# A transformer layer with 32 experts on one core: the skipped general pass and the norm's spread at other experts, chunks taken by pairs of pages

## The chip, the cores and the metric

The kernel runs on one core of a Trainium2 chip. The metric is the device time of one execution in microseconds (us). It has five engines that matter here: TensorE (PE, with its weight loads as PEld), VectorE (DVE), ScalarE (ACT), GpSimd (POOL) and SyncE (SP). In this kernel SP issues every transfer between the outer memory and the core's own memory.

## The reference, cut to what matters

One decoder layer for 256 tokens of width 1024: attention and a gated recurrence, an output projection, a layer norm, then a mixture of 32 experts of which each token takes 4, then a second layer norm. All weights are float32. What bears on the change:

```python
h = layer_norm(DN_ALPHA * h + mix, ln1_g[l], ln1_b[l])
ffn = moe(h, w_router[l], b_router[l], w_gate_up[l], b_gate_up[l], w_down[l], b_down[l])
h = layer_norm(DN_ALPHA * h + ffn, ln2_g[l], ln2_b[l])
# in moe, for each expert e and the rows xb that chose it:
h = xb @ w_gu[e] + b_gu[e]                       # 1024 -> 2 x 1024
act = gate * jax.nn.sigmoid(SWIGLU_ALPHA * gate) * (up + 1.0)
y = act @ w_dn[e] + b_dn[e]                      # 1024 -> 1024, weighted and added per token
```

An expert has 8 MB of gate and up weights and 4 MB of down weights, so the 32 experts read about 403 million bytes, and each byte is used once.

## The kernel before, in words

The first part (projections, attention, recurrence, router) is put in order by a planner with costs and priorities; it ends at about 205 us of the profiled execution. The rest is a plain loop over the 32 experts, written in the order in which each engine runs it. This loop holds the change.

**Pages.** The core's memory for weights is a set of pages of 1 MB. Two neighbouring pages are one tile, called page0 to page12 in the rows; the profile leaves the number out. A queue of wanted loads is drained by `pump`, which is called whenever a buffer is freed while the program is being built. An expert's gate and up weights are eight chunks of 1 MB, g*e*_0 to g*e*_7, its down weights four, d*e*_0 to d*e*_3. In the loop `pump` prefers to load two chunks at once into two neighbouring pages (2 MB, line 436), which needs both pages of a tile to be free; otherwise a chunk goes alone (1 MB, line 451). After the first experts eleven tiles are in turn. SP waits for each load in the order of issue: for the last matmul that reads the old content of the tile, and for the landing of the load eight places earlier, since eight semaphores are shared in turn.

**One turn of the loop for expert e.** `gate_up` (line 1647): four small matmuls for the bias, then eight chunks of eight matmuls, then the gate on DVE and ACT. `down` of the expert before (line 1682): two for the bias, 32 matmuls. `turn` (line 1670) transposes the gated rows, `scatter_lhs` (line 1637) the weighted selection; on odd experts `gather` (line 1620) selects the tokens of the next two experts by matmuls with a 0/1 matrix; `combine` (line 1728) adds the outputs of the expert before into four accumulators. Every matmul goes through the helper at line 488, every transpose through line 495.

**What the change touches.** The first layer norm's gain and bias rows (`ln1`) are spread over the partitions by `spread` (two matmuls each) and applied to `h1` by `gain_bias` (line 1755, four DVE operations) at experts 0 and 1. The residual, `alid` times `h1`, is eight matmuls that start the four accumulators, at expert 1. `count` (line 1798) finds the largest number of tokens of any expert, at expert 0. `fallback` (line 1757) is a general pass for experts with more than 64 tokens, within a branch that all engines take or skip; with these inputs it is skipped. It stands at the last expert, 31, between `combine` of expert 29 and the first half of `gate_up` of 31. The last expert's loads come in pieces of 0.25 to 1 MB.

Of the kernel before, what the change touches and what calls it, by code (L numbers as in the profile page):

```python
# [34 lines left out]
SCRATCH = 1024  # L35
NR = 4
WARM = 30
GATE = {'wq0': 2.75, 'wq1': 5.75, 'wkg0': 8.75, 'wkg1': 11.5, 'wgh0': 14.5, 'wgh1': 17.5, 'wqa0': 20.25, 'wqa1': 23.25, 'wvs0': 26.25, 'wkv0': 29.0, 'wc00': 32.0, 'wc10': 35.0, 'wc01': 37.75, 'wc11': 40.75, 'wi0': 43.75, 'wi1': 46.5, 'wo2': 49.5, 'wo3': 61.75, 'wo0': 64.5, 'wo1': 69.75, 'bias': 86.0, 'xres': 87.5, 'ln1': 90.25, 'g0_0': 91.0, 'g0_1': 94.0, 'g0_2': 101.75, 'g0_3': 104.5, 'g0_4': 107.5, 'g0_5': 110.5, 'g0_6': 113.25, 'g0_7': 118.0, 'g1_0': 122.0, 'g1_1': 124.75, 'g1_2': 127.75, 'g1_3': 130.75, 'g1_4': 137.5, 'g1_5': 140.25, 'g1_6': 143.25, 'g1_7': 151.0, 'd0_0': 153.75, 'd0_1': 156.75, 'd0_2': 159.75, 'd0_3': 167.25}
# [284 lines left out]
def layer(ctx: ExitStack, tc: tile.TileContext, a: dict, out: bass.AP, dbg=None, n_exp=NEXP, cap_limit=CAP):  # L323
# [71 lines left out]
    def want(name, src, shape, kind="pre"):  # L395
        queue.append((name, src, shape, kind))

    def pump():
        while queue:
            name, src, shape, kind = queue[0]  # L400
# [969 lines left out]
    def router_sums():  # L1370

        yield ROUTER_AT
        scratch["late"][0] = Buf(0, key=(qf_late[0], 1024, 1024))
        rsum, gb1, wr1 = (brief(n_, [w], "late") for n_, w in (("rsum", 2 * NEXP), ("gb1", 2 * KD), ("wr1", (KD + 2) * NEXP)))
        wr1v, rsum = shaped(wr1, (KD, NEXP)), shaped(rsum, (2, NEXP))
        h1b.update(rsum=rsum, gb1=gb1, wr1=wr1)
        tmp, ones = brief("rtmp", [KD, NEXP]), brief("ones", [128], "late")
        sums = brief("sums", [2, NEXP], "late")
        pool.memset(ones, 1.0)
        fm = lambda c: col_of(c)[:, :, None].to_broadcast([P, KD, NEXP])  # L1380
        pool.tensor_tensor(tmp, wr, fm(B_B1), OP.mult)
        pool.tensor_tensor(wr1v, wr, fm(B_G1), OP.mult)
        pool.memset(wr1[:, KD * NEXP:], 0.0)
        pool.tensor_copy(gb1, pk[:, B_G1:B_G1 + 2 * KD])
        yield
        dve.tensor_reduce(sums[:, 0, :], tmp.rearrange("p k e -> p e k"), AX.X, OP.add)
# [50 lines left out]
    def norm_route(t):  # L1437
# [76 lines left out]
        h1b[f"tw{t}"] = (ts, tw)  # L1514

    def gather_first(t):

        yield f"rk{t}"
        yield "pm11" if t == 0 else "g0"
        if t == 0:  # L1520
            while (bk := grab(2)) is None:
                yield POLL
            h1b["pg"] = bk
        pg, gb1 = h1b["pg"], h1b["gb1"]
        for k in range(KD):
# [7 lines left out]
        for k in range(KD):  # L1533
            z, o = pg[k // 4][:, (k % 4) * 128:(k % 4 + 1) * 128], h1b["xg"].v(KD, 128)[:, k, :]
            if k % 2:
                act.activation(o, z, AF.Identity, bias=gb1[:, KD + k:KD + k + 1], scale=gb1[:, k:k + 1])
            else:
                dve.tensor_scalar(o, z, gb1[:, k:k + 1], gb1[:, KD + k:KD + k + 1], OP.mult, OP.add)
        drop(*pg)
# [79 lines left out]

    def gather(xg, G):  # L1620

        n = G.shape[2] * CAP
        for q in range(2):
            bk = take(1)
            for t in range(2):
                for k in range(4):
                    mm(bk[0][:, k * 128:k * 128 + n], h1[:, t, (4 * q + k) * 128:(4 * q + k + 1) * 128],
                       G[:, t].rearrange("p e s -> p (e s)"), k == 0 and t == 0, t == 1)
            act.copy(xg[:, 4 * q:4 * q + 4, :n], bk[0].rearrange("p (a b) -> p a b", a=4)[:, :, :n])  # L1629
            drop(*bk)  # L1630
# [15 lines left out]

    def gate_up(xg, wg, i3e, ga, sg_, fs=slice(0, FF)):

        hb = take(2)
        n = (fs.stop - fs.start) // 2  # L1650
        ones_ = i3e.to_broadcast([96, CAP])
        for k in range(-1, KD):
            w_ = wg(k) if k >= 0 else None
            for j in range(2):
                for q in range(2):
# [4 lines left out]
                    else:  # L1660
                        mm(o, xg[:, k, :], w_[j][:, q * n:(q + 1) * n], False, k == KD - 1)
        dve.tensor_scalar(ga, hb[0][:, :n], 7.0, None, OP.min)  # L1662
# [64 lines left out]

    def combine(sz, y):

        for t in range(2):  # L1730
            for q in range(2):
                rows = slice(q * 64, q * 64 + 64)
                mm(acc[t * 2 + q], sz[rows, t, :], y[rows, :], False, False)

# [22 lines left out]
    def fallback():  # L1757

        wb = [buf(2048) for _ in range(3)]
        szb, xb, wkb = buf(512), buf(1024), [buf(512) for _ in range(4)]  # L1760
        sz, xg, (ga, sg_, aT, y) = szb.v(2, 128), xb.v(KD, 128), [z.v() for z in wkb]
        col, wcol, i3e = small("xcol", [2, 1]), small("xwcol", [2, 1]), small("xi3", [1], BF16, 96)
        with tc.If(most > cap_limit):
            with tc.For_i(0, n_exp, 1) as ei:
# [6 lines left out]
                def wg(k):  # L1771
                    w_ = wb[n[0] % 3].v()
                    n[0] += 1
# [3 lines left out]
                def wd(fc):  # L1777
                    if fc % 2 == 0:
                        n[0] += 1
                    w_ = wb[n[0] % 3].v(2, 1024)  # L1780
                    if fc % 2 == 0:
# [38 lines left out]
    def wd_of(e):  # L1820
# [12 lines left out]
        return wd  # L1833

    w0, w1, w2 = [z.v() for z in h1b["wk"]]
    act_, sg_, aTb, y = w0[:, :512], w0[:, 512:], w1, w2
    pump()

    for e in range(n_exp):
        end = e == n_exp - 1  # L1840
        if end:
            most = nc.values_load(cnt[0:1, 0:1], min_val=0, max_val=S)
            fallback()
        sw = weights_of(rk1[:, :, e:e + 1], Wt[:, :, e:e + 1], e % 2)
        pair = e % 2 == 1 and not end
# [6 lines left out]
        else:  # L1852
            wg = wg_of(e)
            gate_up(xg, wg, i3e, act_, sg_)
            done(wg.used.pop())
        if e < 2:
            assert have("ln1")
            spread(loaded["ln1"][1], gain_bias, (2 * e, 2 * e + 1))
        if e == 1:
            done("ln1")  # L1860
        if e == n_exp - 2:
            assert have("ln2")
            lnp = loaded["ln2"][0][0].v(2, D)
            spread(loaded["ln2"][1], lambda c, z: act.copy(lnp[:, c // 2, c % 2 * 512:c % 2 * 512 + 512], z))
        if e:
            wd = wd_of(e - 1)
            down(wd, i3[:, e - 1:e], aT, y)
            done(wd.used.pop())
        else:
            scatter_lhs(swz[0], sw)  # L1870
            count()
        aT = turn(act_[:, :256] if end else act_, aTb[:, :256] if end else aTb)
        if e:
            scatter_lhs(swz[e % 2], sw)
        if e == 1:
            for t in range(2):
                for q in range(2):
                    mm(acc[t * 2 + q], alid, h1[:, t, q * 512:(q + 1) * 512], True, False)
        if pair:
            gather(xgb, G)  # L1880
        if e:
            combine(swz[(e - 1) % 2], y)

# [105 lines left out]
```

## Time and profile before

| what | value |
|---|---|
| median of 3 runs | 1148.53 us (1148.23 to 1149.32) |
| the profiled execution, its own time | 1148.06 us |
| its span, first to last instruction | 1146.3 us |
| PE busy | 1051.5 us (92%) |
| DVE, ACT, POOL busy | 293.7, 199.6, 74.8 us |
| read from the outer memory | 428.05 MB, 374 GB/s over the span |
| transfers that SP issued, share of 16 engines | 89.6% |

The profile cuts the span into 40 slices of 28.66 us and gives for each the bytes per second that the transfers moved. It also lists groups of instructions, the idle time before them and what ended it. Rows are read with the line numbers of the kernel before.

### The profile page before, as it was taken

How to read it: one execution, taken by the hardware profiler on the slowest of the kernel's cores; microseconds unless marked ns; L12 is line 12 of the kernel's file. 1: busy time of each engine (PE TensorE's matmuls, PEld its weight loads, DVE VectorE, ACT ScalarE, POOL GpSimd, SP SyncE). 2: the span in 40 equal slices, each digit the busy share in tenths (PEclk: the TensorE clock that was granted, in tenths of full speed). 3: DMA queues.
4: the chain of work that ended last, by engine and by line, in shares of the span. 5: the costliest groups of instructions: out<-in, count | busy, mean ns of one | idle time of the engine just before them, and what ended most of it. 6: DMA issues, size and time to landing. Idle time of an engine off the chain costs nothing. (4 is left out here: it accounts for less than half of the span.)

```text
span 1146.3 us, 13469 instructions
## 1 busy us (share of the span) xinstructions
PE 1051.5 (92%) x5714; PEld 496.4 (43%) x5714; DVE 293.7 (26%) x625; ACT 199.6 (17%) x418; POOL 74.8 (7%) x70
## 2 busy tenths in 40 slices
PE   9888899899999999999898989898999989898976
PEld 8768577343434343434242423242323333333353
DVE  4897885421111111111111110111111111111103
ACT  5565653100101010101010101000101010101101
POOL 4454220000000000000000000000000000000001
PEclk9998899999999999999999999999999999999988
DMA  9732745997999999999999999999999999999980
GB/s 336 318 148 88 281 169 185 423 409 309 427 428 428 428 428 428 427 427 428 428 427 428 429 426 428 429 426 429 428 427 427 426 429 428 428 428 428 418 341 37
DMA packets 37664, 430.02 MB, mean 375 GB/s; under 512 B 4184, under 2 KB 4440, under 8 KB 9568
## 3 DMA queue, kind: packets, MB, share of 16 engines
q1 hardware_dynamic: 37600, 429.11, 89.6%
q8 instruction: 47, 0.77, 0.3%
q14 instruction: 17, 0.14, 0.0%
HBM read 428.05 MB, written 1.05 MB: 374 GB/s over the span
## 5 line engine op out<-in xcount | busy, mean ns | idle before, releaser
L488 PE MATMUL bank<-page,page 128*64 128x512 f32 (+1 forms) x3160 | 689.3, 587 | 52.8 <-DMA page<-in_w_dn 31.1
L488 PEld LDWEIGHTS bank<-page,page 128*64 128x64 f32 x3160 | 227.9, 138 | 484.0 <-issue 376.7
L1662 DVE TENSOR_SCALAR page<-bank 128x512 f32<-128x512 f32 (+1 forms) x33 | 22.3, 675 | 546.5 <-issue 297.1
L144 PE MATMUL bank<-page,page 128*128 128x256 f32 (+6 forms) x836 | 130.5, 333 | 8.9 <-ACT page L144 4.3
L144 PEld LDWEIGHTS bank<-page,page 128*128 128x128 f32 (+2 forms) x836 | 107.2, 188 | 24.2 <-ACT page L144 6.2
L1663 ACT ACTIVATE page<-page 128x512 f32<-128x512 f32 (+1 forms) x33 | 20.3, 617 | 535.8 <-DVE page L1662 535.8
L1644 DVE COPY page<-bank 128x256 f32<-128x256 f32 x32 | 13.6, 424 | 213.5 <-PE bank L488 202.6
L488 PE MATMUL bank<-page 64*128 64x512 f32 (+2 forms) x260 | 65.8, 608 | 0.9 <-ACT page L1712 0.7
L1899 POOL TENSOR_TENSOR page<-page,page 128x320 f32<-128x320 f32 (+1 forms) x2 | 1.6, 792 | 935.9 <-DVE page L1906 935.9
L1689 ACT COPY page<-bank 128x512 f32<-128x512 f32 x31 | 18.2, 586 | 246.3 <-PE bank L488 246.3
L144 POOL TENSOR_TENSOR page<-page,page 128x512 fp32r<-128x512 f32 (+4 forms) x37 | 55.4, 1512 | 75.4 <-ACT page L144 63.4
L488 PE MATMUL bank<-G,page 128*128 128x128 f32 x480 | 57.5, 278 | 0.0
L144 DVE TENSOR_TENSOR page<-page,page 128x512 fp32r<-128x512 f32 (+6 forms) x58 | 49.0, 879 | 28.8 <-ACT page L144 28.6
L488 PEld LDWEIGHTS bank<-G,page 128*128 128x128 f32 x480 | 54.8, 192 | 2.9 <-issue 2.9
L144 ACT CAST page<-page 128x512 fp32r<-128x512 f32 (+3 forms) x71 | 43.8, 656 | 22.8 <-PE bank L144 13.7
L144 PE MATMUL bank<-page 128*128 128x128 f32 (+4 forms) x182 | 33.7, 329 | 9.4 <-DVE page L144 7.1
L488 PEld LDWEIGHTS bank<-page 64*128 64x128 f32 (+1 forms) x260 | 23.3, 186 | 22.3 <-issue 18.6
L144 PEld LDWEIGHTS bank<-page 128*128 128x128 f32 x182 | 26.4, 200 | 13.4 <-DVE page L144 6.2
L1664 DVE TENSOR_TENSOR page<-page 128x512 f32<-128x512 f32 (+1 forms) x33 | 22.3, 676 | 22.5 <-ACT page L1663 22.5
L1629 ACT COPY page<-bank 128x512 f32<-128x512 f32 x30 | 17.6, 585 | 50.4 <-PE bank L488 50.4
L488 PEld LDWEIGHTS <-i 96*64 96x64 bf16 x197 | 9.0, 108 | 39.9 <-issue 39.6
L495 PEld LDWEIGHTS bank<-cst,page 128*128 128x128 f32 x128 | 13.4, 140 | 27.4 <-issue 25.2
(148 smaller groups left out, 482.8 us busy)
## 6 DMA issues: line engine op xcount, KB each, us to landing
page<-in_w_gu SPq DMA_DIRECT2D x115, 2048.0 KB, 39.1
page<-in_w_dn SPq DMA_DIRECT2D x58, 2048.0 KB, 39.1
page<-in_w_gu SPq DMA_DIRECT2D x18, 1024.0 KB, 7.2
page<-in_w_dn SPq DMA_DIRECT2D x8, 1024.0 KB, 9.1
page<-in_w_gl SPq DMA_DIRECT2D x16, 512.0 KB, 18.7
page<-in_w_o SPq DMA_DIRECT2D x4, 1024.0 KB, 6.0
page<-in_w_dl SPq DMA_DIRECT2D x5, 512.0 KB, 10.1
page<-in_w_q SPq DMA_DIRECT2D x2, 1024.0 KB, 5.8
```

The costliest lines, as they stand in the source:

```text
L144: r = f(*args, **kw)
L488: pe.matmul(o, l, r, start=start, stop=stop, skip_group_check=True)
L495: pe.transpose(o, i_, ident if idn is None else idn)
L1629: act.copy(xg[:, 4 * q:4 * q + 4, :n], bk[0].rearrange("p (a b) -> p a b", a=4)[:, :, :n])
L1644: dve.tensor_copy(sz.rearrange("p a b -> p (a b)"), bk[0][:, :256])
L1662: dve.tensor_scalar(ga, hb[0][:, :n], 7.0, None, OP.min)
L1663: act.activation(sg_, ga, AF.Sigmoid, scale=1.702)
L1664: dve.tensor_tensor(sg_, sg_, ga, OP.mult)
L1689: act.copy(y, py)
L1899: pool.tensor_tensor(z, z, lnp[:, 0, c0:], OP.mult)
```

## The change

Five things change. (1) `fallback` stands at the start of expert 16 instead of 31, with two weight buffers instead of three; from the end of `gate_up` of expert 15 on, `pump` issues nothing until the branch has been placed. (2) `spread` of the first norm's gain and bias is at experts 2 and 3; the gathers for experts 0 to 3 therefore read rows without gain and bias, and `gained` applies both, on DVE and ACT in turn, to the gathered columns. For that the small tile `gb1` keeps its place. (3) `count` is at expert 2. (4) The residual's eight matmuls are at expert 8, and the first `combine` starts the accumulators. (5) At experts 0 to 2 the chunks are taken in an order by pairs of pages: chunks that lie in two neighbouring pages first and together.

```diff
     def pump():
-        while queue:
+        while queue and not held_back:
...
+    def gained(o, z, k):
+
+        gb1 = h1b["gb1"]
+        if k % 2:
+            act.activation(o, z, AF.Identity, bias=gb1[:, KD + k:KD + k + 1], scale=gb1[:, k:k + 1])
+        else:
+            dve.tensor_scalar(o, z, gb1[:, k:k + 1], gb1[:, KD + k:KD + k + 1], OP.mult, OP.add)
...
-    def gather(xg, G):
+    def gather(xg, G, gains=False):
...
-            act.copy(xg[:, 4 * q:4 * q + 4, :n], bk[0].rearrange("p (a b) -> p a b", a=4)[:, :, :n])
+            if gains:
+                for k in range(4):
+                    gained(xg[:, 4 * q + k, :], bk[0][:, k * 128:k * 128 + n], 4 * q + k)
+            else:
+                act.copy(xg[:, 4 * q:4 * q + 4, :n], bk[0].rearrange("p (a b) -> p a b", a=4)[:, :, :n])
...
-        wb = [buf(2048) for _ in range(3)]
+        wb = [buf(2048) for _ in range(FALL)]
         szb, xb, wkb = buf(512), buf(1024), [buf(512) for _ in range(4)]
+        held_back.clear()
...
+    def neighbours(names):
+
+        at = {loaded[nm][0][0].key[0]: i for i, nm in enumerate(names)}
+        return tuple(at[pg] for pg in sorted(at, key=lambda pg: (pg ^ 1 not in at, min(at[pg], at.get(pg ^ 1, 99)), at[pg])))
...
-        if end:
+        if e == min(AT_FALL, n_exp - 1):
             most = nc.values_load(cnt[0:1, 0:1], min_val=0, max_val=S)
             fallback()
+            pump()
...
-            gate_up(xg, wg, i3e, act_, sg_)
+            gate_up(xg, wg, i3e, act_, sg_, ks=neighbours([f"g{e}_{k}" for k in range(KD)]) if e < 3 else range(KD))
             done(wg.used.pop())
-        if e < 2:
+        if e in (2, 3):
             assert have("ln1")
-            spread(loaded["ln1"][1], gain_bias, (2 * e, 2 * e + 1))
-        if e == 1:
+            spread(loaded["ln1"][1], gain_bias, (2 * e - 4, 2 * e - 3))
+        if e == 3:
             done("ln1")
...
+        if e == min(AT_FALL, n_exp - 1) - 1:
+            held_back.append(e)
...
             scatter_lhs(swz[0], sw)
-            count()
...
-        if e == 1:
+        if e == 2:
+            count()
+        if e == min(AT_ALID, n_exp - 1):
             for t in range(2):
                 for q in range(2):
-                    mm(acc[t * 2 + q], alid, h1[:, t, q * 512:(q + 1) * 512], True, False)
+                    mm(acc[t * 2 + q], alid, h1[:, t, q * 512:(q + 1) * 512], False, False)
         if pair:
-            gather(xgb, G)
+            gather(xgb, G, e == 1)
         if e:
-            combine(swz[(e - 1) % 2], y)
+            combine(swz[(e - 1) % 2], y, e == 1)
```

First place: SP's loads from d1_0 to the first two of g4, before. The number behind `page` is the tile, the one behind the underscore its version; `in_w_gu` is a gate and up load, `in_w_dn` a down load.

```order
L451 DMA page2_1386<-in_w_dn 128x2048 x2
L451 DMA page5_71<-in_w_dn 128x2048
L451 DMA page9_75<-in_w_dn 128x2048
L436 DMA page3_69<-in_w_gu 128x4096
L436 DMA page10_76<-in_w_gu 128x4096
L436 DMA page1_1743<-in_w_gu 128x4096
L436 DMA page7_1812<-in_w_gu 128x4096
L436 DMA page4_70<-in_w_dn 128x4096
L436 DMA page6_72<-in_w_dn 128x4096
L436 DMA page8_74<-in_w_gu 128x4096
```

And after, the same stretch.

```order
L456 DMA page2_1386<-in_w_dn 128x2048 x2
L456 DMA page5_71<-in_w_dn 128x2048 x2
L441 DMA page3_69<-in_w_gu 128x4096
L441 DMA page10_76<-in_w_gu 128x4096
L441 DMA page1_1744<-in_w_gu 128x4096
L441 DMA page7_1813<-in_w_gu 128x4096
L441 DMA page6_72<-in_w_dn 128x4096
L441 DMA page8_74<-in_w_dn 128x4096
L441 DMA page0_1321<-in_w_gu 128x4096
```

The second half of d1 goes to the other page of page5 instead of page9, and d2_0 goes to page6 instead of page4. At expert 2 page4 holds g2_1, which before is the second chunk to be used, and page6 holds g2_2 and g2_3, which after are the first two.

Second place: PE between `down` of expert 0 (page7) and the bias of expert 2 (i3), before.

```order
L488 MATMUL bank0_79<-page7_1812,page12_78 64x512 x8
L495 MATMUL bank7_86<-cst_87,page12_78 128x128 x4
L488 MATMUL bank4_83<-cst_87,page12_78 64x128 x4
L488 MATMUL bank6_85<-page11_77,page12_78 128x512
L488 MATMUL bank2_81<-page11_77,page12_78 128x512
L488 MATMUL bank5_84<-page11_77,page12_78 128x512
L488 MATMUL bank3_82<-page11_77,page12_78 128x512
L488 MATMUL bank1_80<-G0_150,page11_77 128x128 x8
L488 MATMUL bank0_79<-G0_150,page11_77 128x128 x8
```

And after.

```order
L493 MATMUL bank1_80<-page7_1813,page12_78 64x512 x8
L500 MATMUL bank7_86<-cst_87,page12_78 128x128 x4
L493 MATMUL bank0_79<-cst_87,page12_78 64x128 x4
L493 MATMUL bank4_83<-G0_150,page11_77 128x128 x8
L493 MATMUL bank1_80<-G0_150,page11_77 128x128 x8
```

The four matmuls with page11 and page12 as inputs, the residual, are gone from here.

Third place: SP around the branch, after, with the semaphores that each row waits for (DMAHW0 to DMAHW7 are the eight of the loads). The rows of the general pass itself, which is skipped, are left out between the two pieces. First the last load ahead of it and the test.

```order
L441 DMA page5_71<-in_w_gu 128x4096 [waits DMAHW6_49,PE_49]
L1862 TENSOR_LOAD cnt_1844 [waits DVE_49]
L1862 ISA x2
L1778 COMPARE_AND_BRANCH
```

Then what SP runs when the pass is skipped, and the first loads behind it.

```order
L1778 UNCONDITIONAL_BRANCH [waits DMAHW0_49,DMAHW1_49,DMAHW2_49,DMAHW3_49,DMAHW4_49,DMAHW5_49,DMAHW6_49,DMAHW7_49]
L441 DMA page3_69<-in_w_gu 128x4096 [waits DMAHW1_49,DMAHW6_49,DVE_49,DMAHW7_49,PE_49,Activation_49]
L441 DMA page10_76<-in_w_dn 128x4096 [waits DMAHW0_49,Activation_49]
L441 DMA page1_1744<-in_w_dn 128x4096 [waits PE_49]
L441 DMA page7_1813<-in_w_gu 128x4096 [waits DMAHW2_49,PE_49]
```

The page5 load is the third quarter of g17, the page3 load the fourth. Before, the same test stands behind the last weight load of the kernel.

## Rows read from the trace of the kernel before

**Rows 1.** Page, part 2: GB/s of the transfers in 40 slices.

```profile
GB/s 336 318 148 88 281 169 185 423 409 309 427 428 428 428 428 428 427 427 428 428 427 428 429 426 428 429 426 429 428 427 427 426 429 428 428 428 428 418 341 37
```

**Rows 2.** Windows: us, each engine's busy time, clock, transfers' share, GB/s.

```profile
260.00:262.00 2.00, 2.00 (x12) 0.70 (x12) 0.00 (x0) 0.00 (x0) 0.00 (x0) 1.00 0.00 0
...
300.00:1050.00 750.00, 701.54 (x3618) 267.39 (x3614) 101.52 (x211) 61.79 (x104) 0.00 (x0) 1.00 1.01 428
```

**Rows 3.** Timeline of SP, 222 to 275 us: start, length, what it issues.

```profile
233.85 16.58 SPq L436 DMA_DIRECT2D page<-in_w_gu  x4
264.40 3.76 SPq L436 DMA_DIRECT2D page<-in_w_dn  x2
```

**Rows 4.** SP's waits, 255 to 266 us: total, times, longest.

```profile
SPq L436 <- PE bank L488: 13.9, 1, 13.9
```

**Rows 5.** Line 436, issue to landing: the load of 250.10, then of 264.40.

```profile
DMA to landing us min/median/max: 9.1/9.1/9.1
...
DMA to landing us min/median/max: 7.7/7.7/7.7
```

**Rows 6.** Timeline of PE, experts 0 to 4.

```profile
223.52 0.66 PE L495 MATMUL bank<-cst,page 128*128 128x128 f32 x4 [1.25 <-DVE page L1755]
224.71 1.06 PE L488 MATMUL bank<-bgu,i 96*64 96x512 bf16 x4 [0.54 <-DVE page L1755]
225.52 15.16 PE L488 MATMUL bank<-page,page 128*64 128x512 f32 x64
...
243.01 7.06 PE L488 MATMUL bank<-page,page 128*64 128x512 f32 x32
...
251.18 3.70 PE L488 MATMUL bank<-page,page 128*128 128x512 f32 x8
254.71 3.73 PE L488 MATMUL bank<-G,page 128*128 128x128 f32 x32
...
260.75 13.90 PE L488 MATMUL bank<-page,page 128*64 128x512 f32 x64
...
313.45 13.90 PE L488 MATMUL bank<-page,page 128*64 128x512 f32 x64
```

**Rows 7.** Timeline of DVE: a gained column block, then expert 0's last gate operation.

```profile
204.41 0.41 DVE L144 TENSOR_SCALAR page<-bank,page 128x128 f32<-128x128 f32 x1 [1.39 <-PE bank L144]
...
221.58 0.69 DVE L1667 SCALAR_TENSOR_TENSOR page<-page 128x512 f32<-128x512 f32 x1
```

**Rows 8.** Line 1763, the branch, on all engines: ns min/median/max, first and last start.

```profile
L1763 SPq EVENT_SEMAPHORE  x8: 17/17/17, 1116.1 to 1117.7; - x8
...
L1763 PEldq COMPARE_BRANCH  x1: 6067/6067/6067, 1085.1 to 1085.1; - x1
...
L1763 SPq COMPARE_BRANCH  x1: 50/50/50, 1108.5 to 1108.5; - x1
```

**Rows 9.** Timeline of PE, experts 28 to 31.

```profile
1046.45 3.65 PE L488 MATMUL bank<-page,page 128*64 128x512 f32 x16 [1.25 <-DMA page<-in_w_dn]
...
1084.84 1.99 PE L488 MATMUL bank<-page 64*128 64x512 f32 x8
1091.32 0.42 PE L488 MATMUL bank<-bgu,i 96*64 96x256 bf16 x4 [4.50 <-PEq L1763]
...
1096.89 8.89 PE L488 MATMUL bank<-page,page 128*64 128x256 f32 x58 [3.92 <-issue]
...
1115.89 0.41 PE L488 MATMUL bank<-bgu,i 96*64 96x256 bf16 x4
1116.13 7.08 PE L488 MATMUL bank<-page,page 128*64 128x256 f32 x64
...
1132.67 1.89 PE L488 MATMUL bank<-page,page 128*64 128x256 f32 x15
```

**Rows 10.** Windows of the same time.

```profile
1091.00:1103.00 12.00, 7.76 (x44) 5.91 (x46) 0.00 (x0) 0.00 (x0) 0.00 (x0) 0.57 0.98 387
```

**Rows 11.** Page, part 6: KB each, median us from issue to landing.

```profile
page<-in_w_gu SPq DMA_DIRECT2D x115, 2048.0 KB, 39.1
```

More of the change, by code (lines that the diff above doesn't have):

```diff
@@ L36 @@
 NR = 4
+FALL = 2
+AT_FALL = 16
+AT_ALID = 8
 WARM = 30
@@ L396, in want @@
         queue.append((name, src, shape, kind))
+    held_back = []
     def pump():
-        while queue:
+        while queue and not held_back:
             name, src, shape, kind = queue[0]
@@ L1373, in router_sums @@
         scratch["late"][0] = Buf(0, key=(qf_late[0], 1024, 1024))
-        rsum, gb1, wr1 = (brief(n_, [w], "late") for n_, w in (("rsum", 2 * NEXP), ("gb1", 2 * KD), ("wr1", (KD + 2) * NEXP)))
+        rsum, wr1 = (brief(n_, [w], "late") for n_, w in (("rsum", 2 * NEXP), ("wr1", (KD + 2) * NEXP)))
+        gb1 = small("gb1", [2 * KD])
         wr1v, rsum = shaped(wr1, (KD, NEXP)), shaped(rsum, (2, NEXP))
@@ L1523, in gather_first @@
             h1b["pg"] = bk
-        pg, gb1 = h1b["pg"], h1b["gb1"]
+        pg = h1b["pg"]
         for k in range(KD):
@@ L1533, in gather_first @@
         for k in range(KD):
[L1534 to L1538, printed above, removed]
+            gained(h1b["xg"].v(KD, 128)[:, k, :], pg[k // 4][:, (k % 4) * 128:(k % 4 + 1) * 128], k)
         drop(*pg)
@@ L1645, in scatter_lhs, with gate_up @@
         drop(*bk)
-    def gate_up(xg, wg, i3e, ga, sg_, fs=slice(0, FF)):
+    def gate_up(xg, wg, i3e, ga, sg_, fs=slice(0, FF), ks=range(KD)):
         hb = take(2)
@@ L1651, in gate_up @@
         ones_ = i3e.to_broadcast([96, CAP])
-        for k in range(-1, KD):
+        for k in (-1, *ks):
             w_ = wg(k) if k >= 0 else None
@@ L1660, in gate_up @@
                     else:
-                        mm(o, xg[:, k, :], w_[j][:, q * n:(q + 1) * n], False, k == KD - 1)
+                        mm(o, xg[:, k, :], w_[j][:, q * n:(q + 1) * n], False, k == ks[-1])
         dve.tensor_scalar(ga, hb[0][:, :n], 7.0, None, OP.min)
@@ L1726, in down_last, with combine @@
         return st
-    def combine(sz, y):
+    def combine(sz, y, first=False):
         for t in range(2):
@@ L1732, in combine @@
                 rows = slice(q * 64, q * 64 + 64)
-                mm(acc[t * 2 + q], sz[rows, t, :], y[rows, :], False, False)
+                mm(acc[t * 2 + q], sz[rows, t, :], y[rows, :], first, False)
     def spread(rows, use, which=range(4)):
@@ L1771, in wg @@
                 def wg(k):
-                    w_ = wb[n[0] % 3].v()
+                    w_ = wb[n[0] % FALL].v()
                     n[0] += 1
@@ L1779, in wd @@
                         n[0] += 1
-                    w_ = wb[n[0] % 3].v(2, 1024)
+                    w_ = wb[n[0] % FALL].v(2, 1024)
                     if fc % 2 == 0:
```

## The prediction

> **What bounds the kernel now.** I read the slices of transfer rate first. From the eleventh slice on they show 427 to 429 GB/s in nearly every slice, whatever the engines do [rows 1], and over 750 us of that stretch the transfers' share is 1.01 while PE, the busiest engine, has 48 us to spare [rows 2]. So from about 270 us the stream of weights sets the time. A pair of chunks (2 MB, 2.097 million bytes) takes 2.097/0.428 = 4.9 us, an expert of six pairs 29.4 us; PE needs (313.45 - 260.75)/2 = 26.35 us for one [rows 6]. Three questions remain: where the stream stands still, what starts it again, and how long the kernel runs on behind its last byte.
>
> The tenth slice has 309 GB/s instead of 428 [rows 1]. The windows inside it show no byte at all from 260 to 262 us [rows 2]. SP issues four pairs from 233.85 on, the last at 250.10, and then nothing until 264.40 [rows 3]; its one wait there is 13.9 us for PE [rows 4]: no pair of pages is free. The load of 250.10 lands 9.1 us later, at 259.2; that of 264.40 takes 7.7 us, to 272.1 [rows 5]. From landing to landing that is 12.9 us where the stream needs 4.9: **8.0 us lost**.
>
> At the end, PE is level with the stream at 1046.45 us (it had waited 1.25 us for that load), and has done with `combine` at 1086.83. Then it stands 4.50 us at the branch of line 1763, does a few matmuls, stands another 3.92 us with nothing to wait for [rows 9], and runs to 1103 at a mean granted clock of 0.57, so mostly at the lower of its two levels, 1.2 instead of 2.4 GHz [rows 10]. The last loads land by 1117.7, when SP passes its eight waits at the branch [rows 8]; PE is still in the second half of the last `gate_up` then, until 1123.2 [rows 9].
>
> **The change part by part: experts 0 to 2.** The late load, d2_0, waits for the first two chunks of expert 2, before as after, only from other pages. So the gap moves with PE's arrival there.
> - Expert 0 loses a `spread` and `count`. Its `turn` waited 1.25 us, and the next bias 0.54, for the DVE work of `gain_bias` [rows 6]; without it `turn` waits for the gate's last DVE operation, which ends at 222.27 [rows 7]. Expert 1 starts 1.8 us earlier, so its chunks start at 223.7 and end at 238.9.
> - Expert 1 loses the other `spread`: from the chunks' end (240.68) to `down` (243.01) are 2.3 us [rows 6], of which 0.2 stay for the bias. Gain 2.1.
> - The residual goes: 254.71 - 251.18 = 3.5 us [rows 6].
>
> Together 7.4 us: expert 2's chunks start at 253.3, two are done 3.5 us later, and d2_0 is issued at 264.40 - 7.4 = 257.0. It then lands 7.7 us later, at 264.7, against 272.1. The load ahead of it ends at 259.2 or a little earlier, so 264.1 is the best the stream could do: 0.6 us of the 8.0 are left.
>
> The chunk order itself gives what keeps this fed: page5 and page10 come free after two and six chunks of expert 1 instead of six and eight, and half of d1 is issued no later than before. What is late next is d3_0, into the page of g3_0 and g3_1. By the same durations `gate_up` of expert 2 ends at 267.2, its new `spread` at 269.4, `down` at 276.6, `turn`, `scatter_lhs`, `count` and `combine` at 280.1; two chunks on, 284.0. It is the sixth pair behind d2_0, so the stream wants it issued by 264.7 + 6 x 4.9 - 7.7 = 286.4. That leaves 2.4 us; behind it the slack grows by some 3 us per expert.
>
> Two costs lie here. The eight `gained` operations replace two ACT copies; nearest is 0.41 us for one on DVE [rows 7]. Four follow the second bank: 1.6 us, within the 1.99 of `combine` [rows 9]. Uncovered they would cost up to 1.6, and nothing below zero. The residual at expert 8 puts 3.7 us on PE, where by then 4 x 3 us of slack exist: nothing. The two spreads only move. I take **-7.4**, with -5.5 and -8.0 (the whole gap) as ends.
>
> **The branch at expert 16.** The skip makes SP wait for all eight load semaphores, as the order shows and as it did at 1116.1 to 1117.7 [rows 8]; there it had nothing left to issue. Now the last quarter of g17 and all that follows is queued behind it, so the stream runs dry once. Held-back loads don't add: up to eight loads, 39.1 us from issue to landing [rows 11], are still out when SP arrives, and PE's own stop of 4.5 + 3.9 us passes meanwhile. When they have landed, PE has long freed the pages of eight further pairs, for it takes 3.5 us for a pair whose transfer takes 4.9. So the cost is one restart: issue-to-landing 7.7 [rows 5], less 4.9 of transfer, is 2.8, plus some 0.4 for SP's last waits and its branch, an estimate from eight waits of 0.02 us and a test of 0.05 [rows 8]. I take **+3.2**. Below 2.8 it can't be, since the bytes are the same and the engines were full; above, SP might stand as PE did: 3.2 + 4.5 + 3.9 = 11.6.
>
> SP's own test took 0.05 us, PE's 6.07, of which 4.50 left the engine idle [rows 8, 9]; so the two differ, and SP can do its fetching during the drain. The Trainium skill (Runtime: NRT & Kernel Launch, section Instruction fetch mechanics) says that a taken branch breaks the sequential prefetch and that execution waits until the target's page has come by a DMA. PE's idle time agrees; by that rule alone, applied to SP after the drain, the cost would be 7.7 instead of 3.2 us. What in these rows would make SP do so is the second rival below.
>
> **The tail.** Without the branch at expert 31, PE goes from `combine` straight into the first half of `gate_up`. It saves 4.5, 3.9, and the slow clock: the first half took 1105.78 - 1091.32 - 3.92 = 10.5 us, the second, alike, 1123.21 - 1115.89 = 7.3 [rows 9]; 3.2 more. Sum **-11.6**. Is the stream late next? In the old times PE would start the second half's loads at about 1105 and end at 1111.7; the kernel's last pieces land until 1117.7 and are wanted for the product that starts 1132.67 - 1123.21 = 9.5 us after that half's end, so at 1121. The slack is 3 us. Bounds: -8.4, where the slow clock stays, and -11.6.
>
> **Sum.** The profiled execution took 1148.06 us, 1.8 us more than its span, 0.5 less than the median. 1148.06 - 7.4 + 3.2 - 11.6 = 1132.3; 0.5 up to the median's level: 1132.8, so **1133 us**. Own range 1130.5 to 1136.
>
> **Rivals.**
> - *The gap comes back one expert on.* If PE reaches d3_0's page 2.4 us later than worked out (a slow clock after expert 0's idle, or uncovered `gained`), the stream stops again there. For it: the slack is small, and the same clock loss cost 15.16 - 13.90 us at expert 1 [rows 6]. Against: that loss is in the sum already. Price about 3.5: 1136.5. Chance 0.13.
> - *SP stands behind the drain.* Its next instructions come late when the queue is already empty, once (4.5) or twice (8.4) as on PE: 1137.5 to 1141.4. Against: it waits tens of us before. Chance 0.10.
> - *The tail keeps its second stop.* The 3.92 us that rows 9 put down to nothing, and the clock after it, belong to that place in the code and not to the branch: 7.1 us are kept, 1140. Against: it comes only 1.65 us of work behind the branch. Chance 0.07.
> - *Slower: PE's skip waits behind the weights.* At expert 16 the queue is full, 39.1 us deep [rows 11]. If each of PE's two stops waited through it, 78 us, the first loads behind the branch, which also wait for PE, would be issued late: PE arrives some 6 us behind SP's last issue (3.7 of `gather` and 2.0 of `combine` [rows 6, 9]), with 33 us of queue left, two pairs with free pages are 10 more, and some 35 us of the stream stay empty: 1133 + 35 = 1168. It ends slower than before once the stream is empty for over 15.7 us more than forecast. Against: at 1085 the queue was busy too, and the stops were 4.5 and 3.9 us. Chance 0.04.
>
> **How the numbers follow.** The forecast has 0.66. Its range and the first two rivals reach from 1130 to 1139.5, without the second rival's dearer half and most of the third; a little room below for a stream that also loses its small pauses ahead of the gap gives 1129.5 to 1139.5. Changes below 0.2% (2.3 us) can't be told from none in this kernel. Faster holds in all cases but the last: 0.94; slower 0.04; the rest, 0.02, for several of them together.
>
> **What would show it.** Right: the tenth slice at about 420 GB/s; one slice near the middle, at expert 16, lower by some 10% (3.2 of 28.7 us); SP's eight waits at the branch in mid-kernel, ended by landings, and the next issue within 0.5 us; no idle PE before the last `gate_up`, and its first half at 7.3 us. Wrong: empty stretches beyond 4 us at expert 16, a new gap near 285 us, or PE waiting for a load behind the last `gate_up`, since then the loads would have become the tail's limit.

## The result and the profile after

Four runs of the changed kernel took 1134.87, 1137.22, 1137.48 and 1137.66 us, median **1137.35 us**, beside 1148.84 us for the kernel before on the same chip: ratio 0.9896, 95% interval 0.9878 to 0.9913. The forecast was 1133 us, range 1129.5 to 1139.5. The profiled execution is the shortest of the four, 1134.87 us with a span of 1133.0.

Where it went is read best by cutting each profile at three starts on PE: the first chunk of expert 0; the last `down` matmuls that PE holds back for a load at expert 29; and the last piece of the last `down`. All but the end of the span are starts in the timeline of PE; the first of the kernel before is

```profile
205.57 13.90 PE L488 MATMUL bank<-page,page 128*64 128x512 f32 x64
```

| us | start of expert 0's chunks | from there to that load ("stream") | from there to the last piece ("tail") | from there to the end | span |
|---|---|---|---|---|---|
| before | 205.57 | 840.88 | 86.22 | 13.63 | 1146.3 |
| after | 204.72 | 837.81 | 75.98 | 14.49 | 1133.0 |
| difference | -0.85 | -3.07 | -10.24 | +0.86 | -13.3 |

The first row of the page to compare is that of the transfer rate in 40 slices, now 28.33 us each; it answers to [rows 1].

```profile
GB/s 329 332 150 88 275 174 174 425 425 425 426 425 427 426 427 426 427 426 427 427 426 428 420 346 428 426 427 427 425 429 427 426 426 428 427 426 426 420 415 118
```

The tenth slice has 425 GB/s instead of 309, the ninth 425 instead of 409: that gap is closed. The twenty-fourth has 346 instead of 426: a new one, at expert 16. The timeline of SP (start, length, what it issues) shows the first, and answers to [rows 3]:

```profile
229.59 14.28 SPq L441 DMA_DIRECT2D page<-in_w_gu  x4
254.39 3.76 SPq L441 DMA_DIRECT2D page<-in_w_dn  x2
...
281.47 3.76 SPq L441 DMA_DIRECT2D page<-in_w_dn  x2
```

The late load d2_0 is issued at 254.39 instead of 264.40, and no load behind it is late: d3_0 goes at 281.47, where the prediction had 284.0 and a limit of 286.4. The timeline of PE says why (idle time and its releaser in brackets; it answers to [rows 6]).

```profile
204.72 13.90 PE L493 MATMUL bank<-page,page 128*64 128x512 f32 x64
...
221.47 0.66 PE L500 MATMUL bank<-cst,page 128*128 128x128 f32 x4 [2.41 <-DVE page L1681]
...
222.51 13.90 PE L493 MATMUL bank<-page,page 128*64 128x512 f32 x64
...
236.47 7.03 PE L493 MATMUL bank<-page,page 128*64 128x512 f32 x32
...
244.61 3.84 PE L493 MATMUL bank<-G,page 128*128 128x128 f32 x32
...
250.75 13.90 PE L493 MATMUL bank<-page,page 128*64 128x512 f32 x64
...
277.82 7.46 PE L493 MATMUL bank<-page,page 128*64 128x512 f32 x34
```

Expert 1's chunks start 17.8 us behind those of expert 0 (before: 225.52 - 205.57 = 19.95), and take 13.90 us instead of 15.16: the slow clock that followed the idle time is gone too (granted clock 1.00 from 225 to 230 us, before 0.70). `down` follows them with no gap, the residual is not there, and expert 2 starts at 250.75 instead of 260.75.

At expert 16 the instructions of the branch (line 1778, on all engines; ns min/median/max, first and last start) answer to [rows 8].

```profile
L1778 SPq EVENT_SEMAPHORE  x8: 17/17/17, 639.4 to 668.8; - x8
...
L1778 SPq COMPARE_BRANCH  x1: 50/50/50, 629.9 to 629.9; - x1
L1778 PEldq COMPARE_BRANCH  x1: 6254/6254/6254, 631.7 to 631.7; - x1
```

SP tests and branches at 629.9 in 0.05 us and then stands in eight waits until 668.8, while its loads land one by one: the drain. The timeline of SP around it:

```profile
618.85 50.53 SPq L441 DMA_DIRECT2D page<-in_w_gu  x4
669.49 0.84 SPq L441 DMA_DIRECT2D page<-in_w_dn  x2
```

The fourth of those four loads is issued at the end of the 50.53 us, less its own 0.33: 669.05, which is 0.25 us behind the last wait. Windows of 2 us show what the stream does meanwhile (columns as in [rows 2]: each engine's busy time, clock, transfers' share, GB/s).

```profile
662.00:664.00 2.00, 2.00 (x18) 1.23 (x18) 0.51 (x2) 1.17 (x2) 0.00 (x0) 1.00 0.91 385
664.00:666.00 2.00, 2.00 (x14) 0.71 (x12) 0.76 (x4) 0.00 (x0) 0.00 (x0) 1.00 0.52 221
666.00:668.00 2.00, 2.00 (x12) 0.66 (x10) 0.00 (x0) 0.00 (x0) 0.00 (x0) 1.00 0.23 98
668.00:670.00 2.00, 2.00 (x12) 0.59 (x10) 0.00 (x0) 0.00 (x0) 0.00 (x0) 1.00 0.03 8
670.00:672.00 2.00, 2.00 (x12) 0.70 (x10) 0.00 (x0) 0.00 (x0) 0.00 (x0) 1.00 1.05 262
```

The queue does not stop at one moment. It runs down over some 6 us (385, 221, 98, 8 GB/s), while the gap of before broke off within one such window:

```profile
256.00:258.00 2.00, 2.00 (x20) 2.00 (x20) 0.00 (x0) 0.58 (x1) 0.00 (x0) 1.00 0.99 426
258.00:260.00 2.00, 2.00 (x13) 0.94 (x11) 0.00 (x0) 0.58 (x1) 0.00 (x0) 1.00 0.07 25
```

PE, meanwhile, passes its own branch:

```profile
638.08 1.06 PE L493 MATMUL bank<-bgu,i 96*64 96x512 bf16 x4 [3.84 <-PEq L1778]
638.91 16.27 PE L493 MATMUL bank<-page,page 128*64 128x512 f32 x64
...
676.82 3.65 PE L493 MATMUL bank<-page,page 128*64 128x512 f32 x16 [0.61 <-DMA page<-in_w_gu]
```

It stands 3.84 us, and the chunks behind take 16.27 instead of 13.90 us (granted clock 0.50 from 638 to 642 us). The second stop of [rows 9] does not follow here. The first load that PE waits for behind the branch is that of 676.82, after the restart, and for 0.61 us.

The tail on PE answers to [rows 9]:

```profile
1042.53 3.65 PE L493 MATMUL bank<-page,page 128*64 128x512 f32 x16 [1.25 <-DMA page<-in_w_dn]
...
1067.26 4.21 PE L493 MATMUL bank<-page,cst 4*128 4x512 f32 x8
...
1071.83 9.67 PE L493 MATMUL bank<-page,page 128*64 128x512 f32 x32
...
1084.53 0.41 PE L493 MATMUL bank<-bgu,i 96*64 96x256 bf16 x4
1084.77 7.08 PE L493 MATMUL bank<-page,page 128*64 128x256 f32 x64
...
1101.97 7.08 PE L493 MATMUL bank<-page,page 128*64 128x256 f32 x64
...
1118.51 1.89 PE L493 MATMUL bank<-page,page 128*64 128x256 f32 x15
```

Nothing is idle in front of the last `gate_up`; its halves take 7.08 us each, and PE waits for no load behind 1042.53. One thing was not foreseen: `down` at 1071.83 takes 9.67 us. Before, the same 32 matmuls took 8.26. The window shows the granted clock after, 0.66, and so mostly the lower of its two levels (1.2 instead of 2.4 GHz):

```profile
1075.47 8.26 PE L488 MATMUL bank<-page,page 128*64 128x512 f32 x32
...
1070.00:1080.00 10.00, 10.00 (x31) 2.79 (x31) 0.18 (x1) 1.17 (x2) 0.00 (x0) 0.66 1.03 413
```

The matmuls ahead of it are those of the second norm's `spread` (1067.26), four rows deep instead of 128; before, they took 3.93 us instead of 4.21.

### The profile page after: what moved, and what is told of

Read it like the earlier page. It is cut to its first block, busy times and chain, and to the rows that moved or that the text cites. A ratio compares the mean times of both kernels' runs of the same rounds, so it can differ in the third digit from the quotient of the medians.

```text
span 1133.0 us, 13479 instructions
## 1 busy us (share of the span) xinstructions
PE 1047.9 (92%) x5714; PEld 490.3 (43%) x5714; DVE 294.3 (26%) x629; ACT 200.1 (18%) x420; POOL 75.4 (7%) x70
## 5 line engine op out<-in xcount | busy, mean ns | idle before, releaser
L493 PEld LDWEIGHTS bank<-page,page 128*64 128x64 f32 x3160 | 223.2, 138 | 474.8 <-issue 385.7
L1676 DVE TENSOR_SCALAR page<-bank 128x512 f32<-128x512 f32 (+1 forms) x33 | 22.3, 675 | 523.6 <-PE bank L493 277.7
L1658 DVE COPY page<-bank 128x256 f32<-128x256 f32 x32 | 13.6, 424 | 209.9 <-PE bank L493 197.3
L147 DVE TENSOR_TENSOR page<-page,page 128x512 fp32r<-128x512 f32 (+6 forms) x58 | 48.9, 879 | 29.2 <-ACT page L147 29.1
L147 ACT CAST page<-page 128x512 fp32r<-128x512 f32 (+3 forms) x71 | 43.5, 654 | 23.4 <-PE bank L147 13.8
## 6 DMA issues: line engine op xcount, KB each, us to landing
page<-in_w_dn SPq DMA_DIRECT2D x8, 1024.0 KB, 11.6
page<-in_w_dl SPq DMA_DIRECT2D x5, 512.0 KB, 10.2
```

Of the source, the lines that this page charges most:

```text
L147: r = f(*args, **kw)
L493: pe.matmul(o, l, r, start=start, stop=stop, skip_group_check=True)
L1658: dve.tensor_copy(sz.rearrange("p a b -> p (a b)"), bk[0][:, :256])
```

## Experiments

### The changed kernel again (e1_again, e10_after)

No edit.

> The changed kernel once more, unaltered. Its first four runs lay at 1134.87 (the profiled one) and at 1137.2 to 1137.7. Theory: the 2.5 us between them come from the clock of TensorE in the tail: in the profiled run the window 1070 to 1080 us had a mean granted clock of 0.66, around the spread of the second norm's rows, and the tail is bound by TensorE. Then a profile near 1137 shows about 2.5 us more of it there, with the stream's last landing at the same time. Rival: the stream itself runs at another rate or starts later; then the last landing is late by the same 2.5 us. Both expect 1134.5 to 1138 us.

> The changed kernel, untouched, as the yardstick for the two kernels beside it on this chip. Both theories: between 1134.2 and 1137.4 us, the two medians that it has had.

Measured: 1134.2 us (1132.8 to 1136.04, 4 runs), ratio 0.9877 [0.9862, 0.9892]; and on another chip 1135.99 us (1134.15 to 1138.51, 5 runs), ratio 0.9895 [0.9877, 0.9912]. All 13 runs of this kernel lie within 1132.8 and 1138.5. The profile of e1_again is of a run of 1133.36 us. It starts at 205.13, and has 837.58 us of stream and 74.29 of tail, 1.7 less than the first profile: `down` behind the second norm's `spread` is faster in it.

```profile
1071.68 8.30 PE L493 MATMUL bank<-page,page 128*64 128x512 f32 x32
```

The profile of e10_after is one of the longer runs, 1138.05 us. Its PE, at the first chunks of expert 0 and at the held-back load of expert 29:

```profile
207.40 13.90 PE L493 MATMUL bank<-page,page 128*64 128x512 f32 x64
```

```profile
1045.67 3.65 PE L493 MATMUL bank<-page,page 128*64 128x512 f32 x16 [1.25 <-DMA page<-in_w_dn]
```

Stream and tail are 838.27 and 75.99 us, as in the first profile (837.81, 75.98). But expert 0 starts 2.7 us later, in the part of the program that the change leaves alone; its window from 40 to 80 us has a granted clock of 0.88, against 0.96 in the shorter run.

```profile
40.00:80.00 40.00, 35.88 (x190) 31.18 (x191) 38.50 (x57) 24.58 (x46) 22.32 (x14) 0.88 0.67 257
```

So some 3 us of the level of one run are decided before the first expert, and 1.7 in the tail. In this longer run the tail's clock, which e1_again was to find at fault, is that of the first profile; the later start, its rival, makes the difference. The profile of before (start at 205.57) was one with little of that.

### The branch alone, and everything but the branch (e3_only_branch, e2_branch31)

e3_only_branch is the kernel before, with only this (cut at the dots; the two places that pick a buffer count to 2 as well):

```diff
-        while queue:
+        while queue and not held_back:
...
-        wb = [buf(2048) for _ in range(3)]
+        wb = [buf(2048) for _ in range(2)]
+        held_back.clear()
...
-        if end:
+        if e == 16:
             most = nc.values_load(...)
             fallback()
+            pump()
...
+        if e == 15:
+            held_back.append(e)
```

> The kernel before with one thing changed: the branch at expert 16, two buffers, loads held back. Theory: 1148.8 + 5.4 - 11.9 = 1142.3 us, with the gap of 8 us at 259 us still there. By the prediction's terms 1148.8 + 3.2 - 11.6 = 1140.4. If the early part and the branch were not independent (a stream that comes late gives the tail more to wait for), more than 1144.

e2_branch31 is the changed kernel with the branch back at the last expert:

```diff
-AT_FALL = 16
+AT_FALL = 31
...
-        if e == min(AT_FALL, n_exp - 1) - 1:
+        if e == AT_FALL - 1 < n_exp - 2:
             held_back.append(e)
```

> The changed kernel with the branch back at expert 31 and nothing held back; all else as changed. Theory from the two traces (the restart at expert 16 cost the stream 5.4 us, the branch in the tail 11.9): 1137.4 - 5.4 + 11.9 = 1143.9 us. By the prediction's own terms (3.2 and 11.6) 1145.8. If the branch's place did not matter, 1137.4.

Measured: the branch alone 1142.49 us (1141.83 to 1143.58), ratio 0.9949 [0.9935, 0.9963]; all but the branch 1142.39 us (1141.55 to 1142.82), ratio 0.9944 [0.993, 0.9958]. With 1134.2 us for the whole change on the same chip, the halves are worth 6.4 and 6.5 us and the two together 14.7, so they add up to within 2 us. Putting the branch back costs 8.2 us, where the prediction's terms give 11.6 - 3.2 = 8.4; moving it alone gains 6.4, where they give the same 8.4 and the theory, with 5.4 for the restart and 11.9 for the tail, 6.5. The page of the branch alone has both holes, the old one in the ninth and tenth slice and the new one in the twenty-fourth:

```profile
GB/s 333 325 149 88 287 166 181 426 389 324 427 429 427 427 427 428 427 428 427 428 427 429 423 344 429 429 427 429 426 429 428 426 430 425 429 427 425 422 416 125
```

By the cut of the first table it has a stream of 845.47 us, 4.6 more than before, and a tail of 75.98. All but the branch has 834.36 and 87.08, and PE's two stops stand again at the last expert:

```profile
1086.55 0.64 PE L493 MATMUL bank<-bgu,i 96*64 96x256 bf16 x4 [4.72 <-PEq L1778]
...
1092.01 8.14 PE L493 MATMUL bank<-page,page 128*64 128x256 f32 x60 [3.97 <-issue]
```

So the stop of 3.9 us with nothing to wait for comes and goes with the branch. At expert 16 it does not come, with the same branch; what makes it at 31 was not found.

### Without the drain (e6_pool, e11_pool)

The skipped pass's loads are issued on GpSimd's queue, so that SP has nothing to settle where it skips them:

```diff
-                    sp.dma_start(w_, a["w_gu"][eds...
+                    pool.dma_start(w_, a["w_gu"][eds...
...
-                    sp.dma_start(w_, a["w_dn"][eds...
+                    pool.dma_start(w_, a["w_dn"][eds...
```

> The changed kernel with the loads inside the skipped general pass put on GpSimd's queue instead of SP's. Then SP has nothing of the pass to account for and need not wait for its own loads when the pass is skipped; TensorE's stop stays. Theory: the stream is not drained at expert 16, no slice in the middle falls below 420 GB/s, and the 5.4 us come back in full: 1132.0 us. By the prediction's size 1134.2. Rival (it was TensorE's stop that cost the stream, not the drain): no change, 1137.4.

> The changed kernel with the skipped pass's loads on GpSimd's queue, so that SP has no drain to wait for at expert 16, now timed beside the changed kernel on one chip. If the drained queue costs what the twenty-fourth slice lacks (5.4 us), it is 4 to 5.5 us faster than the changed kernel beside it; by the prediction's price for the restart, 3.2 us faster.

Measured: 1131.3 us (1128.62 to 1133.09, 5 runs), ratio 0.9848 [0.9833, 0.9864]; again, beside the changed kernel's 1135.99, 1131.19 us (1130.01 to 1132.33), ratio 0.9849 [0.9832, 0.9866]. That is 4.8 us faster. The branch in the first of the two profiles: GpSimd has the waits, at 277.7, long before; SP only tests.

```profile
L1778 POOLq EVENT_SEMAPHORE  x4: 17/43/43, 277.7 to 277.9; - x4
...
L1778 SPq COMPARE_BRANCH  x1: 50/50/50, 630.7 to 630.7; - x1
```

```profile
GB/s 325 339 150 73 277 187 158 423 424 421 426 427 426 426 428 426 427 426 428 426 426 427 422 427 428 426 427 427 426 426 426 429 427 426 427 426 425 416 408 111
```

The twenty-fourth slice is at 427. PE stands 4.18 us at its own branch (3.84 in the changed kernel), so none of the 4.8 us is PE's. By the cut, the streams are 834.69 and 834.91 us against 837.81 and 838.27 in the changed kernel: **3.1 and 3.4 us** at the load that PE waits for, though the slice lacks (428 - 346)/428 x 28.33 = 5.4 us of bytes. So my expectation, which took the 5.4 for the price, was too high, though the time itself came nearer to it than to 3.2: another 0.9 us of the 4.8 is the end (13.56 and 13.65 us against 14.49 and 14.54), and the start differs too (207.40 and 206.15 us in the two profiles beside each other). Whether the end has to do with the edit isn't shown; it is longer in five of the eight profiles with the drain, and in none of the others.

### The residual (e5_alid1)

The eight matmuls at expert 1 again, where they start the accumulators as before. The first norm's gain and bias are not applied to `h1` until experts 2 and 3, so the residual of this kernel leaves both out; it has the same matmuls at the old place, and is used for its time alone.

```diff
-AT_ALID = 8
+AT_ALID = 1
...
-                    mm(acc[t * 2 + q], alid, h1[:, t, q * 512:(q + 1) * 512], False, False)
+                    mm(acc[t * 2 + q], alid, h1[:, t, q * 512:(q + 1) * 512], True, False)
...
-            combine(swz[(e - 1) % 2], y, e == 1)
+            combine(swz[(e - 1) % 2], y)
```

> The changed kernel with the residual's eight matmuls back at expert 1, where they start the accumulators as before; the rows there have no gain and bias yet, so the residual lacks both. Theory: TensorE reaches expert 2 later by 3.5 us, the load d2_0 is issued at 254.4 + 3.5 = 257.9 instead of 254.4 and lands at 265.6, where the stream alone would have it at 263.5: 2.1 us, so 1139.4 us. Rival (3.5 us go through in full): 1140.9. Rival (hidden): 1137.4.

Measured: 1137.96 us (1136.67 to 1138.43), ratio 0.991 [0.9895, 0.9926]. The changed kernel was not run on that chip; the next kernel's 1134.81 was. PE and SP of the profile, and the window ahead of the landing:

```profile
245.11 3.70 PE L493 MATMUL bank<-page,page 128*128 128x512 f32 x8
248.65 3.73 PE L493 MATMUL bank<-G,page 128*128 128x128 f32 x32
```

```profile
258.33 3.76 SPq L441 DMA_DIRECT2D page<-in_w_dn  x2
```

```profile
258.00:260.00 2.00, 2.00 (x12) 0.70 (x10) 0.00 (x0) 0.00 (x0) 0.00 (x0) 1.00 0.52 98
```

d2_0 is issued at 258.33 instead of 254.39, the tenth slice falls to 376 GB/s, and the stream is 840.80 us long: 3.0 us over the first profile of the changed kernel. That lies between the 2.1 us of the theory and the 3.5 of its first rival, which is also what the prediction gave to the residual; the time is 3.2 us over the 1134.81. The residual's place is a real part of the closed gap.

### The spread and the chunk order (e9_spread01, e4_natural)

```diff
-        if e in (2, 3):
+        if e < 2:
-            spread(loaded["ln1"][1], gain_bias, (2 * e - 4, 2 * e - 3))
-        if e == 3:
+            spread(loaded["ln1"][1], gain_bias, (2 * e, 2 * e + 1))
+        if e == 1:
             done("ln1")
...
-            gather(xgb, G, e == 1)
+            gather(xgb, G)
```

> The changed kernel with the spread of the first norm's rows back at experts 0 and 1 (and no gained gather for experts 2 and 3); residual at 8, branch at 16, count at 2. Theory: TensorE reaches expert 2 later by 1.8 + 2.1 = 3.9 us, of which the stream's slack of 1.5 us hides a part: 2.4 us, so 1139.8 us. Rival (hidden): 1137.4.

Measured: 1134.81 us (1134.21 to 1135.73), ratio 0.988 [0.9865, 0.9895], no slower than the changed kernel: the theory's 1139.8 fell. PE does lose the time:

```profile
225.29 15.62 PE L493 MATMUL bank<-page,page 128*64 128x512 f32 x64
...
257.27 13.90 PE L493 MATMUL bank<-page,page 128*64 128x512 f32 x64
```

Expert 2 starts at 257.27, 6.5 us later than in the changed kernel (1.2 of it from the start), and expert 1's chunks have the slow clock again. But the stream does not see it:

```profile
250.06 11.18 SPq L441 DMA_DIRECT2D page<-in_w_dn  x2
```

The first load of this row is d2_0, at 250.06. It no longer waits for expert 2: in this program it goes to page7, which held the second half of expert 0's down weights, and `down` of expert 0 reads that until 250.03:

```profile
242.99 7.04 PE L493 MATMUL bank<-page,page 128*64 128x512 f32 x32
```

The load that waits for expert 2 is now the next pair, d2_2 and d2_3, at 260.91 (250.06 + 11.18 - 0.33), 4.9 us later in the stream. The rotation of the pages has moved by one, and the chunk order has a part in that. The norm's rows lie in one page of page9. With the spread at experts 0 and 1 they are done with early, and by the order of pairs the other page of page9 does not go to a quarter of d1 as it does before; so the whole tile is free for expert 3, and each load behind gets the tile of the one before it. What was worked out for one load holds only for the page that it happens to get.

The chunk order:

```diff
-ks=neighbours([f"g{e}_{k}" for k in range(KD)]) if e < 3 else range(KD)
+ks=neighbours([f"g{e}_{k}" for k in range(KD)]) if e < 0 else range(KD)
```

> The changed kernel with the chunks of experts 0 to 2 in their natural order. Theory (the gap moves with TensorE's arrival at expert 2, the order only feeds): within 1 us of the changed kernel, so 1136.4 to 1138.4, and the first load behind expert 0 to 1's pages still issued at about 254.5 us. Rival (the order by pairs closes the gap): a gap of 3.5 us, two chunks' time, comes back: 1141.

Measured: 1135.26 us (1134.63 to 1136.25), ratio 0.9885 [0.9869, 0.99], against 1134.2 on the same chip: no difference that can be told. The stream is 837.54 us. In this program d2_0 goes to page4 as before, and is issued at 256.28, 1.9 us later than in the changed kernel, by which this run also starts later. With the spread moved, the chunk order is worth nothing here; and with the chunk order, the spread's place is worth nothing. Each may stand in for the other: both undone at once, with the residual left at expert 8, was not tried.

### The slow clock of the second norm (e7_ln2_early, e8_both)

```diff
-        if e == n_exp - 2:
+        if e == 24:
             want("ln2"...
...
-        if e == n_exp - 2:
+        if e == 26:
             assert have("ln2")
```

> The changed kernel, with the rows of the second norm loaded at expert 24 and spread at expert 26 instead of at expert 30, where PE waits for the stream anyway. Theory: PE sets the tail from the load of 1042.5 us on, so taking 4.2 us of matmuls and 1.7 us of slow clock out of it gives 2 to 4 us (the lower end if PE then waits for loads, as it does for 3.5 us in the kernel with both changes). Rival: the stream, which is late by the restart, sets the tail as soon as PE is earlier, and the time stays within 1 us.

Measured: 1132.05 us (1130.97 to 1133.87), ratio 0.9857 [0.9841, 0.9872], 3.9 us faster than the changed kernel's 1135.99 beside it. The tail is 72.72 us instead of 75.99, 3.3 of the 3.9 us; the stream is no shorter (839.10 us, 838.27 beside it), and the rest is start and end. PE now waits for loads in the tail, which caps the gain:

```profile
1074.97 3.65 PE L493 MATMUL bank<-page,page 128*64 128x512 f32 x16 [1.01 <-DMA page<-in_w_dn]
...
1090.06 3.65 PE L493 MATMUL bank<-page,page 128*64 128x512 f32 x16 [0.88 <-DMA page<-in_w_dn]
1094.99 3.65 PE L493 MATMUL bank<-page,page 128*64 128x512 f32 x16 [1.27 <-DMA page<-in_w_dn]
```

e8_both has this edit and that of e6_pool.

> As the kernel with the skipped pass's loads on GpSimd's queue, and with the second norm's rows loaded ahead of expert 24 and spread at expert 26 instead of 30, where TensorE waits for loads anyway. Theory: the tail is bound by TensorE from the last load of expert 28 on, so its 4.0 us of spread and the slow clock around it (1.4 to 3 us) leave the tail, less some 0.8 us until the loads of expert 29's down weights are late: 1137.4 - 5.4 - 4.5 = 1127.5 us. Rival (the loads become the tail's limit at once): 1132.

Measured: **1129.1 us** (1128.16 to 1129.77), ratio 0.9831 [0.9818, 0.9845], the best version of this study, beside 1131.3 us for e6_pool on the same chip, and between the theory's 1127.5 and the rival's 1132. It has the shorter stream (834.90) and the shorter tail (73.05), and PE's waits from 1060 us on (total, times, longest) show that the stream bounds the tail now, up to the last of them at 1090.59 us:

```profile
PE bank L493 <- DMA page<-in_w_dn: 3.5, 3, 1.3
```

## Why the prediction was right, and by how much its terms were off

**The gap, forecast -7.4.** The mechanism was as described: d2_0 waits for the first two chunks of expert 2. PE gave more than forecast, 10.0 us at expert 2: 0.85 from the start, 2.2 at expert 0, 1.3 for a slow clock that did not come back, 2.2 at expert 1, 3.5 for the residual. The stream could take only its loss: 8.0 us in the tenth slice and 1.3 in the ninth, the "small pauses ahead of the gap". Against it stands a rate that nothing had announced. In the slices 11 to 22 the mean is 427.7 GB/s before and 427.6 with the branch alone, but 426.4 to 426.8 in each of the eleven profiles in which the gap is closed or nearly so; 0.26% of some 780 us is 2.0. At the load that PE waits for, the closed gap is worth 840.88 - 834.69 = 6.2 us without the drain, and 845.47 - 837.81 = 7.7 with it. So -7.4 was a good size, partly by luck: the 0.6 us of gap that it left and the 1.3 of the ninth slice, which it did not count, nearly cancel against the rate. The 3.9 us that the sum gave to the two spreads aren't shown: undone alone, neither their place nor the chunk order cost anything that could be measured, since a page's place in the rotation decided as much as PE's time. The prediction had the chunk order as feeding the stream only, and did not see that it can move the load that waits.

**The restart, forecast +3.2.** Right in kind: eight waits ended by landings, the next issue 0.25 us later, PE's 3.84 us spent within the drain. SP did not stand behind the drain, so the second rival fell. The Trainium skill (Runtime: NRT & Kernel Launch, section Instruction fetch mechanics) has a taken branch wait for a fetch where its target lies outside the two pages at hand. The trace shows no such wait for SP behind the drain, where the next issue is 0.25 us behind the last semaphore; whether SP's target lay outside, no run shows. In size it is 3.1 and 3.4 us where the gap is closed, 4.6 where it isn't. The sign, a slice "lower by some 10%", was too small: it was 19%, because the working left out that the queue runs down before it is empty. A hole of 5.4 us of bytes costs PE only about 3.3, and the traces show where the rest went. From the start of the matmuls that PE holds back at expert 29 to the end, the transfers still move 29.3 MB in the first profile (324 GB/s over 90.47 us) and 29.2 to 29.4 in all eight with the drain, but 28.5 MB in e6_pool (318 over 89.54) and 28.3 to 28.5 in all four that have neither drain nor early gap. So without a drain some 0.9 MB of later loads, 2.1 us of the stream, have been moved ahead of the load that PE needs; behind a drain they haven't, and 5.4 - 2.1 is 3.3. The kernel before, whose queue ran empty once in the early gap, lies between, at 28.8 MB, 0.5 MB or 1.2 us from the kernel with the branch alone, and there the restart costs 4.6.

**The tail, forecast -11.6.** In e1_again, e4_natural and e5_alid1 the tail is 74.3 us: -11.9. In the profile after, and five others with the branch away from 31, it is 76.0: -10.2. The two differ in the lower clock behind the second norm's `spread`, 1.7 us. That was the item missing from the sum, a stretch of thin matmuls that had been there before and of which the prediction said nothing. The third rival, a stop that belongs to the place in the code, fell: without the branch PE doesn't stop there. Nor does it wait for a load.

**The sum.** Forecast for the profiled execution: 1132.3; measured 1134.87. The 2.6 us are the stream (-3.07 instead of -4.2: 1.1), the tail (1.4), the end (0.9) and the start (-0.85). The median lies another 2.5 higher. The three runs behind it left no trace; the profile of 1138.05 us shows how such a run comes about: 2.7 us of later start. The step that failed is the last one, "0.5 up to the median's level": one profile's start and clock were taken for the level of all runs. The median of 1137.35 us lies above the sum's own range of 1130.5 to 1136, and inside the stated one because that had been widened for the first two rivals, neither of which came; so far the hit is luck. The later medians of the same kernel, 1134.2 and 1135.99 us, lie inside both.

**The other rivals.** The gap did not come back at expert 3; d3_0 was issued at 281.47, 4.9 us ahead of the prediction's limit of 286.4; by the same working from d2_0's landing as it was, at 263.6, the slack is 3.8 us instead of 2.4. PE's skip did not wait behind the full queue: 3.84 us at expert 16, 4.50 before at 31.

## What to carry to other kernels

When the stream of weights sets the time, cut every profile where PE waits for a load: the parts ahead, between and behind can then be forecast and checked apart, and the noise of the start falls out. A skipped branch that holds transfers makes their queue settle its semaphores; put it where the queue is idle, or its transfers on a queue that has nothing else to do. Before calling a wait the cause, look at which page it is for: an edit elsewhere can turn the rotation by one and move the wait. Then undoing one of two edits alone can cost nothing though the two together matter.

## What the runs showed of the hardware

The deep queue that was cut off at expert 16 ran down over some 6 us (385, 221, 98, 8 GB/s in windows of 2 us); the short one of the early gap broke off within one window (426, then 25). With a deep queue some 0.9 MB more of later loads had been moved at the start of the held-back matmuls of expert 29 than in the kernels with the drain. The same branch stopped PE once, for 3.7 to 4.2 us, at expert 16 (eleven profiles), and twice, 4.5 to 4.7 and 3.9 to 4.0 us, at expert 31 (two profiles). The rate of a stream that is full throughout was 426.4 to 426.8 GB/s in eleven profiles, 427.6 to 427.7 in the two that have the early gap, for no cause that was found: neither the branch, the chunk order, the spread nor the residual, undone alone, brought it back. And the end of the kernel, from the last piece of `down`, takes 14.5 us in five of the thirteen profiles and 13.6 to 13.8 in the others. The last transfer to the outer memory is issued 10.6 us behind that piece in all of them; from issue to landing it takes, in the first profile of the changed kernel and then in that of e6_pool,

```profile
DMA to landing us min/median/max: 3.0/3.0/3.0
...
DMA to landing us min/median/max: 2.0/2.0/2.0
```

It is 3.0 us in all five, and 2.0 in six of the other eight (in two the trace lacks this landing); why it is one or the other was not found.
